# The head of a transformer block: two token tiles multiplied before they are normalised

## The chip, the cores and the metric

The kernel runs on one core of one Trainium2 chip. The metric is the device time of one execution in microseconds (us). Five engines work side by side, each through its own list of instructions in order: TensorE (PE, matrix products and transposes; its weight loads are listed as PEld), VectorE (DVE), ScalarE (ACT), GpSimd (POOL) and SyncE (SP, which here issues most DMA transfers). They wait for each other by semaphores.

## The reference, cut to what matters

One layer of a hybrid block over 1024 tokens of width 1024. Everything that it multiplies first is the RMS-normalised input `h`:

```python
def rmsnorm(x, g):
    xf = x.astype(jnp.float32)
    y = xf * lax.rsqrt(jnp.mean(xf * xf, axis=-1, keepdims=True) + EPS)
    return (y * g.astype(jnp.float32)).astype(x.dtype)
...
    h = rmsnorm(x, norm_g[l])
    proj = h @ w_in[l]
    q, k, v, za, u, vs, zs, gm = jnp.split(proj, IN_SPLITS, axis=-1)
    ...
    sgo = chunked_spatial_gating(jax.nn.gelu(u, approximate=False),
                                 jax.nn.gelu(vs, approximate=False), ...)
```

`h` is x times a gain per column (`norm_g`) times a factor per token (one over the root of the token's mean square). The factor per token can be applied to a row of `h @ w` after the product as well as to the row of `h` before it. The kernel begins with the columns `vs` of the projection.

## The kernel before, in words

Products are made in f32r: each operand is split into a high part, rounded to f32r (a cast on ACT), and a low part, the rest (a subtraction on DVE), and three of the four products of parts are summed in PSUM: high by high, high by low, low by high. A product instruction here is 128 x 128 by 128 x 512.

**The head** is the stretch up to the first large products. Tokens come in eight tiles of 128 (`x[0]` to `x[7]`), loaded by `load_x` into a ring of three buffers (`wr`). `normed_tile(t)` makes a tile of `h`, turned so that the width lies on partitions:

- `scale_of(t)` squares and sums a tile on ACT (L531), and `rstd_of` takes five small steps on DVE (L133 to L145) with a root on ACT between (L135);
- for each half of the width (`j`), L545 on DVE multiplies the tile by the factors and the gain, four transposes on PE (L551) turn it into a PSUM bank (`ps_tp`, two of them), ACT casts the high part (L554), DVE subtracts the low part (L555), and ACT copies the unsplit values (L558, for tile 0 L615) to the places `f11`, `f21`, `f12`, `f22`. From these the sums of a fast (Winograd) scheme are formed later.

The gain is one row, spread over the partitions by two f32 products with ones (L505) into `g_in`, two PSUM banks. `keep_busy` gives PE products of no use (L498) while nothing has arrived.

`vs_gemm(t)` multiplies a tile by the first 512 columns of the `vs` weights: four quarters of weights of 512 KB (`load_vs(c)`, `split_vs(c)`: L582 and L583 for the first, L155 and L156 for the others), 24 products L596 into one bank (`ps_mm`), and L597 on ACT copies the bank to `xh`. Tiles run one after the other: all four quarters for tile 0, then all for tile 1, and so on. `normed_tile(t + 3)` is written behind `vs_gemm(t)`.

Then **the second pass**: the other 512 columns of `vs`, quarter by quarter, each for all eight tiles in eight banks (`vs_step`, 192 products L565). Its weights take `load`, cast and subtraction through the rings `wr`, `wh` and `wl`. `make_forms` builds the operands `t1` to `t4` from the unsplit values beside it, `gelu_of` applies GELU to `xh`. Behind the second pass stand four products for row sums, and then the long sequence of `gemm_pair` (products at L341) that makes up most of the kernel.

**Order.** The text gives a program order; a scheduler then orders each engine's list by its own estimates of when things are ready, so instructions of one tile stand among those of another. `after(second, first)` pins two instructions of one engine. The lists are fixed when the kernel is built: an engine never passes over an instruction that waits. DMA transfers issued by SP go out in SP's order; a load into a ring buffer waits until the readers of what was there have finished.

Of the kernel before, what the change touches and what calls it, by code (L numbers as in the profile page):

```python
# [52 lines left out]
def hybrid_tile(  # L53
# [16 lines left out]
    nc = tc.nc  # L70
# [59 lines left out]
    def rstd_of(ss, scale, base=EPS, n=1):  # L130

        ve = mtile([P, n], F32, f"st{n}", 16 if n == 1 else 5)
        nc.vector.tensor_scalar(ve[:], ss, scale, base, op0=ALU.mult, op1=ALU.add)  # L133
# [11 lines left out]
        nc.vector.tensor_mul(e[:], e[:], r0[:])  # L145
        return e

    def split(hi, lo, src, minus=False):
        if minus:
            nc.scalar.mul(hi, src, -1.0)  # L150
            nc.vector.scalar_tensor_tensor(
                lo, src, -1.0, hi.bitcast(F32), op0=ALU.mult, op1=ALU.subtract
            )
        else:
            nc.scalar.copy(hi, src)  # L155
            return nc.vector.tensor_sub(lo, src, hi.bitcast(F32))  # L156
# [75 lines left out]
    def half_of(half):  # L232
        return slice(half * HALF, (half + 1) * HALF)
# [256 lines left out]
    x_in = {0: load_x(0)}  # L490
    junk = mtile([P, D], F32, "wl", 3)

    ones_r = slot("b22l", (P, HALF))
# [2 lines left out]
    def keep_busy(n):  # L496
        for _ in range(n):
            nc.tensor.matmul(idle[:], ones_r[:, 0:P], ones_r[:], start=True, stop=True)  # L498

    idle = bank("sc")  # L500
    keep_busy(2)

    g_in = [bank("o") for half in range(2)]
    for half in range(2):
        nc.tensor.matmul(g_in[half][:], plain[0:1, 0:P], g_row[:, half_of(half)], start=True, stop=True)  # L505
# [20 lines left out]
    casts = []  # L526

    def scale_of(t):
        xt = x_in[t] if t in x_in else load_x(t)
        ss = mtile([P, 1], F32, "st1", 16)  # L530
        square = nc.scalar.activation(junk[:], xt[:], AF.Square, accum_out=ss[:])  # L531
        if t == 1:

            after(square, casts[-1])
        return xt, rstd_of(ss[:], 1.0 / D)

    def normed_tile(t, scale=None):
        xt, r = scale or scale_of(t)
        if t == 4:
            hb.update(new_b(("b22",)))  # L540
            f.update((n, slot(at, dt=F32)) for n, at in (("f12", "t4h"), ("f22", "t3h")))
        turned = []
        for j in range(2):
            cs = half_of(j)
            nc.vector.scalar_tensor_tensor(  # L545
                xt[:, cs], xt[:, cs], r[:], g_in[j][:], op0=ALU.mult, op1=ALU.mult
            )
            pt = bank("tp")
            for i in range(4):
                k = j * 4 + i  # L550
                nc.tensor.transpose(pt[:, i * P : (i + 1) * P], xt[:, k * P : (k + 1) * P], ident[:])  # L551
            p3 = pt[:].rearrange("p (k c) -> p k c", k=4)
            hi, lo = quarter_of(t, j)
            casts.append(nc.scalar.copy(hi, p3))  # L554
            nc.vector.tensor_sub(lo, p3, hi.bitcast(F32))  # L555
            turned.append((f[f"f{j + 1}{t // 4 + 1}"][:, :, tokens(t)], p3))
            if t:
                nc.scalar.copy(*turned.pop())  # L558
        return turned

    def vs_step(acc, t, k, wh, wl):

# [5 lines left out]
    vs_w = []  # L568

    def load_vs(c):  # L570
        nc.sync.dma_start(vs_raw[c // 2][:, c % 2, :], w[W_VS + c])

    def split_vs(c):

        raw = vs_raw[c // 2][:, c % 2, :].rearrange("p (k n) -> p k n", k=2)
        hi, lo = (v[c // 2][:, 2 * (c % 2) : 2 * (c % 2) + 2, :] for v in vs_split)
        if c:
            split(hi, lo, raw)
        else:

            for k in range(2):
                nc.scalar.copy(hi[:, k, :], raw[:, k, :])  # L582
                (nc.gpsimd if k else nc.vector).tensor_tensor(  # L583
                    lo[:, k, :], raw[:, k, :], hi[:, k, :].bitcast(F32), op=ALU.subtract
                )
        vs_w.extend((hi[:, k, :], lo[:, k, :]) for k in range(2))

    def vs_gemm(t):
        acc = bank("mm")
        for c in range(4):  # L590
            for n in range(3):
                for k in (2 * c, 2 * c + 1):
                    hi, lo = (v[:, k % 4, :] for v in quarter_of(t, k // 4))
                    wh, wl = vs_w[k]
                    lt, rt = ((hi, wh), (hi, wl), (lo, wh))[n]
                    nc.tensor.matmul(acc[:], lt, rt, start=k == 0 and n == 0, stop=k == KC - 1 and n == 2)  # L596
        nc.scalar.copy(xh[:, t, 0:HALF], acc[:])  # L597

    unsplit = normed_tile(0)
    keep_busy(0)  # L600
# [4 lines left out]
    split_vs(0)  # L605
    x_in[1] = load_x(1)
    split_vs(1)
    second = scale_of(1)
    for c in (2, 3):
        load_vs(c)  # L610
    x_in[2] = load_x(2)
    for c in (2, 3):
        split_vs(c)
    for dst, src in unsplit:
        nc.scalar.copy(dst, src)  # L615
    normed_tile(1, second)
    normed_tile(2)
    for t in range(NT):
        vs_gemm(t)
        if t + 3 < NT:  # L620
            normed_tile(t + 3)


    def vs_weights(c):
# [9 lines left out]

    def gelu_of(t):
        two = xh[:, t : t + 2, 0:HALF]
        after(nc.scalar.activation(two, two, AF.Gelu), casts[-1])
        for i in range(2):
            statistics(t + i, 0)

# [38 lines left out]

    mix_w = mtile([P, KC, P], F32, "wT", 1, pool)  # L680
    nc.sync.dma_start(mix_w[:], sg_w)
    nc.vector.memset(mix_w[64:128, :, 0:64], 0.0)
    ones = mtile([P, P], F32R, "ones", 1, pool)
# [1062 lines left out]
```

## Time and profile before

| | us |
|---|---|
| median of 3 runs | 922.93 (922.37 to 922.99) |
| the profiled execution | 923.07 |
| its span | 921.3 |
| PE busy | 904.7 |
| DVE busy | 691.5 |
| ACT busy | 521.8 |
| POOL busy | 126.8 |

The profile is one execution recorded by the hardware. Its page gives busy times and the chain of work that ended last, followed back from the last instruction; the trace behind it answers with timelines (start, length, engine, line, operation, output and inputs, count; in brackets how long the engine had been idle and what ended that) and with waits. Times count from the span's start. Matmuls are pipelined: the length of one is longer than the distance to the next, so pace is read from starts. The granted TensorE clock of the profiled execution is 0.995 of full speed over the span.

### The profile page before, as it was taken

What the parts mean: (1) busy time and instruction counts of PE and PEld (TensorE: products, weight loads), DVE (VectorE), ACT (ScalarE), POOL (GpSimd) and SP (SyncE); (2) the same over time, 40 slices, a digit from 0 to 9 for tenths busy, and PEclk for the clock granted to TensorE, in tenths of its full rate; (3) what the DMA queues carried; (4) which work ended last, traced back from release to release, by engine and by line L of the source; (5) the groups of instructions that cost most, each with busy time, mean ns of one, the idle gap of its engine ahead of it and who ended that gap; (6) DMA issues with size and microseconds to landing.
All of it is one profiled execution on the core that took longest, in us unless ns stands there. A gap on an engine that the chain in (4) does not pass through costs nothing.

```text
span 921.3 us, 13177 instructions
## 1 busy us (share of the span) xinstructions
PE 904.7 (98%) x4332; PEld 752.7 (82%) x4332; DVE 691.5 (75%) x1241; ACT 521.8 (57%) x1046; POOL 126.8 (14%) x188
## 2 busy tenths in 40 slices
PE   8999999999999999999999999999998999999996
PEld 5888888888888788888888888888877887878885
DVE  6875776656687668887778888747798589579996
ACT  6862443334444366767766766755665385367443
POOL 0002122213011001211101111101100111110012
PEclk9999999999999999999999999999999999999998
DMA  6427678877788676776786799689869755998632
GB/s 240 138 91 215 207 197 184 161 158 234 230 290 267 229 200 182 169 202 184 197 240 222 248 220 253 174 313 349 294 219 341 240 201 151 272 307 303 206 115 114
DMA packets 128734, 201.71 MB, mean 219 GB/s; under 512 B 12345, under 2 KB 60729, under 8 KB 128666
## 3 DMA queue, kind: packets, MB, share of 16 engines
q1 hardware_dynamic: 109512, 148.17, 48.8%
q0 software_dynamic: 19008, 52.44, 23.8%
q8 instruction: 34, 0.56, 0.3%
q14 instruction: 34, 0.28, 0.1%
q10 hardware_dynamic: 146, 0.27, 0.1%
HBM read 144.07 MB, written 86.11 MB: 250 GB/s over the span
## 4 chain that ended last, share of the span: by engine, by line
PE 85%; DVE 8%; DMA 4%; issue 2%; ACT 1%; SPq 1%; DVEq 0%; ACTq 0%
PE ps_mm L341 34%; PE ps_o L341 25%; PE ps_mm L596 5%; PE ps_sc L1076 3%; PE ps_o L1161 2%; PE ps_tp L341 2%; PE ps_tp L1120 2%; PE ps_sc L341 2%; PE ps_tp L764 2%; DVE wl L156 1%; PE ps_tp L565 1%; PE ps_sc L565 1%; PE ps_o L565 1%; PE ps_mm L565 1%; DVE bq L185 1%
## 5 line engine op out<-in xcount | busy, mean ns | idle before, releaser
L155 ACT CAST wh<-s 128x1024 fp32r<-128x1024 f32 (+1 forms) x78 | 78.1, 1005 | 87.2 <-PE ps_mm L341 49.9
L156 DVE TENSOR_TENSOR wl<-wr,wh 128x1024 fp32r<-128x1024 f32 (+1 forms) x80 | 75.7, 948 | 49.1 <-ACT wh L155 48.3
L155 ACT CAST wh<-wr 128x1024 fp32r<-128x1024 f32 (+1 forms) x80 | 66.3, 830 | 71.6 <-PE ps_mm L341 34.3
L156 DVE TENSOR_TENSOR wl<-s,wh 128x1024 fp32r<-128x1024 f32 (+1 forms) x78 | 90.9, 1166 | 9.3 <-ACT wh L155 9.2
L341 PE MATMUL ps_o<-T_t1h,wh 128*128 128x512 f32 x148 | 58.9, 398 | 0.8 <-ACT wh L155 0.7
L341 PE MATMUL ps_o<-T_b22h,wh 128*128 128x512 f32 x148 | 58.2, 394 | 0.0
L341 PE MATMUL ps_o<-T_t1h,wl 128*128 128x512 f32 x148 | 57.9, 391 | 0.3 <-DVE wl L156 0.3
L341 PE MATMUL ps_o<-T_b22l,wh 128*128 128x512 f32 x148 | 57.9, 391 | 0.0
L341 PE MATMUL ps_o<-T_b22h,wl 128*128 128x512 f32 x148 | 57.8, 390 | 0.0
L341 PE MATMUL ps_o<-T_t1l,wh 128*128 128x512 f32 x148 | 57.6, 390 | 0.0
L341 PE MATMUL ps_mm<-T_b11h,wl 128*128 128x512 f32 x140 | 54.8, 392 | 2.9 <-DVE wl L156 2.9
L341 PE MATMUL ps_mm<-T_t4h,wh 128*128 128x512 f32 x140 | 55.3, 395 | 0.5 <-DVE x L376 0.5
L341 PE MATMUL ps_mm<-T_t3l,wh 128*128 128x512 f32 x140 | 54.6, 390 | 0.6 <-DVE T_t3l L156 0.6
L341 PE MATMUL ps_mm<-T_t2h,wl 128*128 128x512 f32 x140 | 55.0, 393 | 0.0
L341 PE MATMUL ps_mm<-T_t2l,wh 128*128 128x512 f32 x140 | 55.0, 393 | 0.0
L341 PE MATMUL ps_mm<-T_b11h,wh 128*128 128x512 f32 x140 | 54.9, 392 | 0.0
L341 PE MATMUL ps_mm<-T_t3h,wh 128*128 128x512 f32 x140 | 54.9, 392 | 0.0
L341 PE MATMUL ps_mm<-T_t2h,wh 128*128 128x512 f32 x140 | 54.7, 391 | 0.0
L341 PE MATMUL ps_mm<-T_t4h,wl 128*128 128x512 f32 x140 | 54.7, 391 | 0.0
L341 PE MATMUL ps_mm<-T_t3h,wl 128*128 128x512 f32 x140 | 54.7, 390 | 0.0
L341 PE MATMUL ps_mm<-T_b11l,wh 128*128 128x512 f32 x140 | 54.6, 390 | 0.0
L1089 ACT ACTIVATE pr<-ps_sc,sm 128x192 f32<-128x192 f32 (+2 forms) x128 | 50.9, 410 | 6.5 <-DVE sm L1085 5.5
(356 smaller groups left out, 2399.6 us busy)
## 6 DMA issues: line engine op xcount, KB each, us to landing
wr<-in_w_dram SPq DMA_DIRECT2D x86, 256.0 KB
sums<-in_w_dram POOLq DMA_DIRECT2D x20, 512.0 KB, 5.6
s<-sums SPq DMA_DIRECT2D x20, 512.0 KB
q_hl<-qhl SPq DMA_DIRECT2D x16, 512.0 KB
q<-q_hl SPq DMA_DIRECT2D x64, 128.0 KB
wr<-in_w_dram SPq DMA_DIRECT2D x14, 512.0 KB
y_dr<-x POOLq DMA_DIRECT2D x28, 256.0 KB, 6.6
g<-in_w_dram POOLq DMA_DIRECT2D x12, 512.0 KB, 7.2
```

The costliest lines, as they stand in the source:

```text
L155: nc.scalar.copy(hi, src)
L156: return nc.vector.tensor_sub(lo, src, hi.bitcast(F32))
L185: op(dst[:, i : i + 2, :], a[:, i : i + 2, :], c[:, i : i + 2, :])
L341: nc.tensor.matmul(acc, lt, rt, start=fresh and k == 0 and n == 0, stop=k == 3 and n == 2, skip_group_check=True,)
L565: mm = nc.tensor.matmul(acc, lt, rt, start=k == 0 and n == 0, stop=k == KC - 1 and n == 2)
L596: nc.tensor.matmul(acc[:], lt, rt, start=k == 0 and n == 0, stop=k == KC - 1 and n == 2)
L764: nc.tensor.matmul(pm[:, t * P : (t + 1) * P], xh[:, half * 4 + t, g * P : (g + 1) * P], bias[-1][1][:, g % 4, :], start=True, stop=True,)
L1076: nc.tensor.matmul(sc[:, i, k0:], q_of[:, c, i * P : (i + 1) * P], kt[:, f, k0:], start=f == 0, stop=f == 1,)
L1089: nc.scalar.activation(held_in[c, i], sc[:, i, lo:hi], AF.Exp, bias=nmax[:, c, i : i + 1], scale=-1.0, accum_out=sums[:, c, i : i + 1],)
L1120: nc.tensor.transpose(dst, pr[:, i, block * P : block * P + width], ident[:])
L1161: nc.tensor.matmul(po[:, cs], lt, rt, start=n == 0, stop=n == len(terms) - 1)
```

## The change

The transposes, splits and products of tiles 0 and 1 no longer wait for the tokens' factors. What is turned is `x` itself; the gain, now per partition (`g_cols`, from eight rows of `norm_g` turned on PE), is multiplied in as DVE takes the turned tile from PSUM (`unscaled`). That product is stored unsplit at `f11` and `f21`, and split into the buffers `b12`, which tiles 4 to 7 use later. The products with the `vs` weights are therefore without the tokens' factors; `nc.scalar.mul(xh..., acc, r)` applies these at the copy out of the bank. Tiles 0 and 1 share each quarter of weights in turn, in two banks. Later (`rescaled`, written behind the products of tiles 3 and 4) the stored product is multiplied by the tokens' factors, spread over partitions by an f32 product of ones and a diagonal (`ones32`, `diag`), and split, to give `h` of tiles 0 and 1 for all that follows.

Also: the gain for tiles 2 to 7 is loaded as 128 equal rows into SBUF (`g_in`, 512 KB); the order of loads is x[0], first weights, x[1], second and third weights, gain, x[2], fourth weights; x[0], x[1] and the gain use the ring `wh`; the order of the three products is high by high, low by high, high by low; the first weights' low parts are all on DVE; seven `keep_busy` products come in a row in place of four; a memset of `mix_w` goes from DVE to POOL; the order on ACT and DVE is partly pinned (`in_row`).

```diff
-    g_row = mtile([P, D], F32, "wh", 3)[0:1, :]
-    nc.scalar.dma_start(g_row, norm_g.partition_broadcast(1))
+    g_rows = mtile([P, D], F32, "wl", 3)[0:KC, 0:P]
+    nc.scalar.dma_start(g_rows, norm_g.rearrange("(k p) -> k p", p=P))
...
-    keep_busy(2)
-
-    g_in = [bank("o") for half in range(2)]
-    for half in range(2):
-        nc.tensor.matmul(g_in[half][:], plain[0:1, 0:P], g_row[:, half_of(half)], start=True, stop=True)
-    keep_busy(2)
+    keep_busy(5)
...
+    def turn(t, j):
+
+        pt = bank("tp")
+        for i in range(4):
+            k = j * 4 + i
+            nc.tensor.transpose(pt[:, i * P : (i + 1) * P], x_in[t][:, k * P : (k + 1) * P], ident[:])
+        return pt[:].rearrange("p (k c) -> p k c", k=4)
...
+    def unscaled(t, j):
+
+        p3, v = turn(t, j), whole(t, j)
+        hi, lo = b12[2 * t + j]
+        in_row("D", nc.vector.tensor_mul(v, p3, g_cols[:, 4 * j : 4 * j + 4].unsqueeze(2).broadcast_to([P, 4, P])))
+        yield
+        in_row("A", nc.scalar.copy(hi, v))
+        in_row("D", nc.vector.tensor_sub(lo, v, hi.bitcast(F32)))
+
+    def rescaled(t, r):
+
+        diag = htile([P, P], F32, "diag")
+        after(nc.vector.tensor_scalar_mul(diag[:], ident[:], r[:]), last_of["N"])
+        rb = bank("o")[:, 0:P]
+        nc.tensor.matmul(rb, ones32[:], diag[:], start=True, stop=True)
+        for j in range(2):
+            v = whole(t, j)
+            nc.vector.tensor_mul(v, v, rb.unsqueeze(1).broadcast_to([P, 4, P]))
+            split(*quarter_of(t, j), v)
...
     def normed_tile(t, scale=None):
...
-                xt[:, cs], xt[:, cs], r[:], g_in[j][:], op0=ALU.mult, op1=ALU.mult
+                xt[:, cs], xt[:, cs], r[:], g_in[:, cs], op0=ALU.mult, op1=ALU.mult
...
+    def vs_part(acc, t, c):
+
+        for n in range(3):
+            for k in (2 * c, 2 * c + 1):
...
+                lt, rt = ((hi, wh), (lo, wh), (hi, wl))[n]
+                nc.tensor.matmul(acc, lt, rt, start=k == 0 and n == 0, stop=k == KC - 1 and n == 2)
...
     load_vs(0)
-    load_vs(1)
...
+    nc.sync.dma_start(x_in[1][:], x[P : 2 * P, :])
+    for c in (1, 2):
         load_vs(c)
+    nc.sync.dma_start(g_in[:], norm_g.partition_broadcast(P))
     x_in[2] = load_x(2)
...
+    load_vs(3)
...
+    raws = [unscaled(t, j) for t in range(2) for j in range(2)]
+    parts = split_vs(0)
+    next(raws[0])
+    next(raws[1])
+    keep_busy(2)
+    next(parts)
+    next(raws[0], 0)
+    next(parts, 0)
+    next(raws[1], 0)
+    scales = [scale_of(0)]
+    firsts = [bank("mm") for _ in range(2)]
+    vs_part(firsts[0][:], 0, 0)
+    next(raws[2])
+    next(raws[3])
+    next(raws[2], 0)
+    next(raws[3], 0)
+    vs_part(firsts[1][:], 1, 0)
+    for c in range(1, 4):
+        next(split_vs(c))
+        for t, acc in enumerate(firsts):
+            vs_part(acc[:], t, c)
+    scale = scale_of(2)
+    scales.append(scale_of(1))
+    for t, acc in enumerate(firsts):
+        nc.scalar.mul(xh[:, t, 0:HALF], acc[:], scales[t][1][:])
+        normed_tile(t + 2, None if t else scale)
+    normed_tile(4)
+    for t in range(2, NT):
+        acc = bank("mm")
+        for c in range(4):
+            vs_part(acc[:], t, c)
+        nc.scalar.copy(xh[:, t, 0:HALF], acc[:])
         if t + 3 < NT:
             normed_tile(t + 3)
+        if t in (3, 4):
+            rescaled(t - 3, scales[t - 3][1])
```

In the changed kernel the squares are at L532, the scaling of tiles 2 to 7 at L583, the transposes at L548, the gain products at L559, the products of the first pass at L625 and of the second at L596.

More of the change, by code (lines that the diff above doesn't have):

```diff
@@ L488, in load_x, with htile @@
         return xt
-    x_in = {0: load_x(0)}
+    def htile(shape, dt, tag):
+        return mtile(shape, dt, tag, 1, pool)
+    x_in = {t: mtile([P, D], F32, "wh", 3) for t in range(2)}
+    nc.sync.dma_start(x_in[0][:], x[0:P, :])
+    ones32 = htile([P, P], F32, "ones32")
+    nc.gpsimd.memset(ones32[:], 1.0)
+    g_in = mtile([P, D], F32, "wh", 3)
     junk = mtile([P, D], F32, "wl", 3)
@@ L524, in quarter_of @@
         return [v[:, :, tokens(t)] for v in hb[("b11", "b21", "b22")[j if t < 4 else 2]]]
-    casts = []
     def scale_of(t):
@@ L541, in normed_tile @@
             f.update((n, slot(at, dt=F32)) for n, at in (("f12", "t4h"), ("f22", "t3h")))
-        turned = []
         for j in range(2):
@@ L545, in normed_tile @@
             nc.vector.scalar_tensor_tensor(
-                xt[:, cs], xt[:, cs], r[:], g_in[j][:], op0=ALU.mult, op1=ALU.mult
+                xt[:, cs], xt[:, cs], r[:], g_in[:, cs], op0=ALU.mult, op1=ALU.mult
             )
[L548 to L552, printed above, removed]
-            hi, lo = quarter_of(t, j)
[L554 to L559, printed above, removed]
+            p3 = turn(t, j)
+            hi, lo = quarter_of(t, j)
+            nc.scalar.copy(hi, p3)
+            last_of["N"] = nc.vector.tensor_sub(lo, p3, hi.bitcast(F32))
+            last_of["A"] = nc.scalar.copy(whole(t, j), p3)
     def vs_step(acc, t, k, wh, wl):
@@ L603, in hybrid_tile @@
     load_vs(0)
-    load_vs(1)
[L605 to L609, printed above, removed]
+    nc.sync.dma_start(x_in[1][:], x[P : 2 * P, :])
+    for c in (1, 2):
         load_vs(c)
+    nc.sync.dma_start(g_in[:], norm_g.partition_broadcast(P))
     x_in[2] = load_x(2)
[L612 to L619, printed above, removed]
+    load_vs(3)
+    g_cols = htile([P, KC], F32, "g_cols")
+    pt = bank("tp")
+    nc.tensor.transpose(pt[:, 0:KC], g_rows, ident[0:KC, 0:KC])
+    in_row("D", nc.vector.tensor_copy(g_cols[:], pt[:, 0:KC]))
+    raws = [unscaled(t, j) for t in range(2) for j in range(2)]
[30 more added lines that the diff above has]
+        nc.scalar.copy(xh[:, t, 0:HALF], acc[:])
         if t + 3 < NT:
             normed_tile(t + 3)
+        if t in (3, 4):
+            rescaled(t - 3, scales[t - 3][1])
     def vs_weights(c):
@@ L636, in gelu_of @@
         two = xh[:, t : t + 2, 0:HALF]
-        after(nc.scalar.activation(two, two, AF.Gelu), casts[-1])
+        after(nc.scalar.activation(two, two, AF.Gelu), last_of["A"])
         for i in range(2):
@@ L681, in hybrid_tile @@
     nc.sync.dma_start(mix_w[:], sg_w)
-    nc.vector.memset(mix_w[64:128, :, 0:64], 0.0)
-    ones = mtile([P, P], F32R, "ones", 1, pool)
+    nc.gpsimd.memset(mix_w[64:128, :, 0:64], 0.0)
+    ones = mtile([P, P], F32R, "ones32", 1, pool)
     nc.vector.tensor_scalar(ones[:], ident[:], 0.0, 1.0, op0=ALU.mult, op1=ALU.add)
```

40 lines of the change are left out of this document (18 added, 22 removed).

## The prediction

> **What bounds the kernel now.** I read the page first, then the chain of waits from its start, then the timeline of the first 20 us engine by engine.
>
> ```profile
> span 921.3 us, 13177 instructions
> PE 904.7 (98%) x4332; PEld 752.7 (82%) x4332; DVE 691.5 (75%) x1241; ACT 521.8 (57%) x1046; POOL 126.8 (14%) x188
> ```
>
> TensorE (PE) has work in 98% of the span, so time can only be won where it waits. The chain of waits shows where that is at the head.
>
> ```profile
> 3.99 3.71 PE ps_o L505 x4
> 7.70 0.52 issue
> 8.21 1.94 PE ps_tp L551 x8
> ...
> 18.11 3.70 PE ps_mm L596 x15
> ...
> 62.30 2.72 PE ps_mm L565 x12
> ...
> 103.10 2.72 PE ps_tp L565 x12
> ```
>
> Columns are start, length, what. The first useful PE work is the transposes at 8.21. From 18.11 the chain holds nothing but PE: the head's products (L596) end at 62.30, and the 192 products of the second pass (L565) end at 103.10 + 2.72 = 105.82, at 2.72/12 = 0.227 us each. In the built order of the changed kernel every engine's list after that point is that of before. So I work out when the changed kernel reaches the end of these 192 products; the difference to 105.82 carries to the end unchanged, as later starts hang on the same PE products and copies.
>
> The head in the timeline:
>
> ```profile
> 1.92 2.07 PE L498 MATMUL ps_sc<-T_b22l 128*128 128x512 f32 x4 [1.92 <-DVE T_b22l L494]
> 4.43 1.06 ACT L531 ACTIVATE wl<-wr 128x1024 f32<-128x1024 f32 x1 [1.64 <-DMA wr<-in_x_dram]
> 5.61 0.15 DVE L133 TENSOR_SCALAR st<-st 128x1 f32<-128x1 f32 x1 [3.75 <-ACT wl L531]
> 5.97 1.14 ACT L582 CAST T_t1h<-T_t3h 128x512 fp32r<-128x512 f32 x2
> 6.68 0.16 DVE L145 TENSOR_TENSOR st<-st,st 128x1 f32<-128x1 f32 x1
> 7.37 1.40 DVE L545 SCALAR_TENSOR_TENSOR wr<-wr,st,ps_o 128x512 f32<-128x512 f32 x2
> 7.99 1.05 ACT L155 CAST T_t1h<-T_t3h 128x1024 fp32r<-128x1024 f32 x1 [0.89 <-DMA T_t3h<-in_w_dram]
> 8.21 1.94 PE L551 MATMUL ps_tp<-ident,wr 128*128 128x128 f32 x8 [0.52 <-issue]
> 9.34 0.59 ACT L554 CAST T_b11h<-ps_tp 128x512 fp32r<-128x512 f32 x1 [0.30 <-PE ps_tp L551]
> 9.97 1.22 PE L596 MATMUL ps_mm<-T_t1h,T_b11h 128*128 128x512 f32 x2
> 10.22 0.68 DVE L555 TENSOR_TENSOR T_b11l<-ps_tp,T_b11h 128x512 fp32r<-128x512 f32 x1
> 10.82 0.68 DVE L555 TENSOR_TENSOR T_b21l<-ps_tp,T_b21h 128x512 fp32r<-128x512 f32 x1
> 12.18 0.62 PE L596 MATMUL ps_mm<-T_t1h,T_b11h 128*128 128x512 f32 x2
> 12.64 0.62 PE L596 MATMUL ps_mm<-T_t1l,T_b11h 128*128 128x512 f32 x2
> 12.80 1.23 DVE L156 TENSOR_TENSOR T_t2l<-T_t4h,T_t2h 128x1024 fp32r<-128x1024 f32 x1 [0.79 <-ACT T_t2h L155]
> ```
>
> Read three things. Tile 0 (x[0]) is in SBUF at 4.43, but its transposes wait until 8.21 for its square, the small DVE steps and the scaling L545. One pass of DVE over 512 columns takes 0.60 (10.22 to 10.82), one over 1024 about 1.2. And PE runs at half pace until about 11.5: four fills in 2.0 us, 0.5 apart, eight transposes from 8.21 to 9.97, 0.22 apart, while from 12.18 two products take 0.46 (0.228 each).
>
> **The change, step 1: the start.** It removes L545 for tiles 0 and 1 and the wait for their squares ahead of the transposes. It adds on DVE, before the first products of tile 1, a chain in this built order: gain times transposed tile 0 (two passes), low part of the first weights, of tile 0, of the next weights, of tile 0, one small step, tile 1's pass, small, tile 1's pass, small, tile 1's low part. PE has 7 fills instead of 4: 1.92 + 7 x 0.5 = 5.4, 0.1 for the transposed gain, then tile 0's eight transposes at 0.22 to 7.3. DVE follows the first four as ACT did before (8.21 to 9.34, 1.13): passes start at 6.6 and 7.5. From 7.5 on stand eight passes of 0.6 and three small steps, 0.2 each with the gap, until tile 1's first low part is there: 7.5 + 8 x 0.6 + 3 x 0.2 + 0.1 = 13.0. PE meanwhile has tile 1's transposes when x[1] lands; it is now the third load, and the third of before was there at 7.99. Three of them stand ahead of the first product, which comes near 8.7 instead of 9.97. So the start wins 1.3 us, but at 13.0 PE has done only 8 of the first 48 products: DVE is the bound of this stretch, no longer the square. From there PE has 40 products in a row, the loads being ahead (below): 13.0 + 40 x 0.228 = 22.1. Call it t0: both first tiles multiplied.
>
> Load order: the last quarter of the weights (the eighth load) comes after the gain for 128 partitions and x[2]. Loads of 512 KB pass at 389 GB/s; while the bias, also one row for all partitions, passes, it is 187:
>
> ```profile
> 19.50:20.50 1.00, 1.00 (x6) 0.81 (x5) 0.81 (x5) 1.00 (x3) 0.00 (x0) 1.00 0.98 389
> 20.50:22.00 1.50, 1.50 (x10) 1.16 (x9) 1.46 (x4) 0.42 (x1) 0.00 (x0) 1.00 0.56 187
> ```
>
> The third load is there at 7.99, so the eighth at 7.99 + 5 x 1.35 = 14.7, or 16.1 with the gain at half rate. PE wants its high part at t0 - 12 x 0.228 = 19.4 and ACT needs 1.05: cover of 2 us, cost nothing; landing later than 18.3 would cost PE one for one.
>
> **Step 2: the other tiles.** What the change moves and does not name: in the new ACT order the square of tile t+1 stands behind the two casts and two copies of tile t, and the transposes of t+1 wait for it. Before, PE turned each tile well ahead of need. Rows for that loop:
>
> ```profile
> 16.78 1.20 PE L551 MATMUL ps_tp<-ident,wr 128*128 128x128 f32 x8
> 16.98 0.59 ACT L597 COPY xh<-ps_mm 128x512 f32<-128x512 f32 x1 [1.16 <-PE ps_mm L596]
> 17.46 0.59 ACT L554 CAST T_b11h<-ps_tp 128x512 fp32r<-128x512 f32 x1
> 18.09 0.69 DVE L555 TENSOR_TENSOR T_b11l<-ps_tp,T_b11h 128x512 fp32r<-128x512 f32 x1 [0.82 <-ACT T_b11h L554]
> 18.11 0.73 PE L596 MATMUL ps_mm<-T_t1h,T_b11h 128*128 128x512 f32 x2
> ...
> 34.23 0.63 PE L551 MATMUL ps_tp<-ident,wr 128*128 128x128 f32 x4
> 34.89 0.59 ACT L554 CAST s<-ps_tp 128x512 fp32r<-128x512 f32 x1 [0.25 <-PE ps_tp L551]
> ```
>
> The cast starts 0.66 after the transposes (34.23, 34.89); ACT passes of 512 columns are 0.48 apart (16.98, 17.46); DVE's low part follows its cast at 0.63. From square to next transposes, by tile 0 of before: 4.43 to 6.68, 0.19 to the end of L145, and from L545 to the transposes 7.37 to 8.21, 0.84: 3.28. Followed with these, from t0:
> - Tile 2 is turned only at t0, as tile 1 was at 16.78. PE waits for copy and cast until t0 + 1.31 (18.11 - 16.78 = 1.33 before), of which transposes fill 0.8, then 0.15 for the low part, which the new order hi.wh, lo.wh, hi.wl asks for after two products instead of four: 0.6 lost.
> - ACT: copies of tile 2 until t0 + 3.13, square of tile 3 there, its transposes not before t0 + 6.41; PE gets to them at 6.38. The second half waits 0.3 for L583.
> - Tile 4's square at t0 + 9.89, transposes from 13.17, PE there at 12.85: 0.3 lost. Tile 5's at 16.61, 19.89, PE there at 19.63: 0.3. Tiles 6 and 7 have products of the second pass in front of them in the order and lose 0.2.
>
> Sum 1.7 us of waits. Each turn of the loop is about 6.7 us against 24 x 0.228 + 1.0 = 6.4 of PE work.
>
> **Step 3: the stored product times the factors.** For each of two tiles a 128 x 128 diagonal (DVE 0.2), one f32 product of 128 columns, two DVE passes, two casts, two low parts. The f32 product is on PE: L505 took 3.71/4 = 0.93 per piece of 512 columns at half pace, two pieces each, so 128 columns are 0.23 at full pace; with weight loads I take 0.4 (bounds 0.2 and 0.9), two: 0.8. DVE 2 x (2 x 0.6 + 2 x 0.6) = 4.8 and ACT 2 x 2 x 0.5 lie beside PE's products of tiles 6 and 7: by my following, tile 0's parts are there at t0 + 35 and first read at t0 + 40; tile 1's at 45 and 48. Cost nothing; without that cover PE would wait for the difference.
>
> **The sum.** After t0: 144 products at 0.228 and 192 at 0.227, 76.4; six tiles turned at (62.30 - 18.11 - 168 x 0.228)/6 = 0.98, 5.9; waits 1.7; f32 products 0.8: 84.8. End 22.1 + 84.8 = 106.9 against 105.82: +1.1. The profiled execution took 923.07 us, 921.3 of it span; the median of the three runs, 922.93, lies 0.14 below. So 924.1 there, 924.0 as a time, likely between 923.0 and 925.0. A measurement of this kernel tells about 0.2%, 1.85 us, from no change.
>
> **Where the clock comes in.** The pace of PE doubles near 11.5, though it had been at work from 1.92 to 7.70 with fills and the gain's one-row products, and waited only 0.52. The Trainium skill ("TensorE: Matmul & The Clock Gate", Part 1) says that about 3.4 us of sustained matmuls release the full clock, by a window that runs free. The trace agrees from 8.21 on (3.3 us), and does not for 1.92 to 7.70. The changed kernel fills with 128-row products from 1.92 into the transposes, so by that rule it could be at full pace by about 5.5. What that gives from rows: transposes at 0.1, DVE passes from 6.15 and 6.75 instead of 7.5, t0 = 21.4, end 106.2.
>
> **The rivals.**
> - Full pace early: 923.2, +0.3. For it: no one-row products are left. Against: the 2.0 us of 128-row fills before did nothing visible. Chance 0.22.
> - Slower, the loop: the square-to-transposes path is on PE's path in tiles 3, 4, 5 and partly 7, so each 0.1 us that I have it too short costs 0.4. It decides from 0.3 us longer: 924.0 + 1.2 = 925.2; at 0.5 longer 926.0. For it: ACT and DVE are strictly in order and weights' casts stand between; the load of w behind tile 5 lands with almost no slack. Against: durations are from undisturbed rows. Chance 0.30.
> - Faster: PE finds its tiles scaled as before (no step 2 waits beyond the first 0.6: -1.1), full pace early (-0.7), f32 products at 0.2 (-0.4), and DVE's gain passes overlapping more with the low parts (-0.7): 921.1. For it: chain of before shows no waits once tiles run ahead. Against: the new ACT order. Chance 0.13.
> - That the change doesn't do what it says: the built order has the transposes ahead of any scaling, so no chance is kept.
>
> **How the numbers follow.** The forecast, half pace until about 11.5 and 1.7 of waits, has 0.35; it and early pace lie within 0.2% of 922.93. Of the loop's 0.30 nearly all is over 924.78, with none of the rest. Of the faster case about all is under 921.08. Range for 8 in 10: from 921.3, just short of the faster case, to 926.2, the loop at 0.55 longer.
>
> **What would show it.** Right: first L625 product near 8.7; tile 1's first low part (x) near 12.3 to 13.0, and PE waiting for DVE before it; both first tiles done near 22; PE waits ahead of the transposes of tiles 3 to 5 named L583; second pass done near 106.9. Wrong: transposes at 0.1 before 8 us, or waits ahead of transposes missing or over 0.6, or a stretch after 107 us whose length is not that of before.

## The result, and the profile after

The changed kernel took 928.89 us (median of 4 runs, 927.11 to 929.69) where the kernel before took 922.96 (4 runs, 922.37 to 923.65): 1.0053 times as long, 95% interval 1.0039 to 1.0068. The forecast was 924.0 with a range up to 926.2, so it is wrong by 4.9 us, and the kernel became slower than the range allowed for. The profiled execution took 928.54 us.

The page of the changed kernel shows the same picture as before, with 5.5 us more span and PE as busy as it was:

```profile
span 926.8 us, 13193 instructions
PE 905.4 (98%) x4336; PEld 754.0 (81%) x4336; DVE 697.5 (75%) x1252; ACT 522.8 (56%) x1046; POOL 126.5 (14%) x189
```

The chain of waits from 10 us on (start, length, what) shows the difference:

```profile
10.59 10.84 DMA sink_sb<-in_sinks_dram
...
21.52 0.09 DVE nsink_sb L772
21.61 0.04 issue
21.66 0.75 DVE wr L583
...
23.28 0.64 PE ps_tp L548 x4
23.92 0.02 issue
23.94 0.69 ACT xh L664
24.62 0.48 ACT T_b11h L588
25.11 0.04 issue
25.15 4.91 PE ps_mm L625 x13
```

In the kernel before, this chain held nothing but PE from 18.11 on. Now a transfer stands in it that neither the diff nor the prediction speaks of: the load of the sinks, 16 numbers that attention needs after 300 us. DVE negates them in L772 (L718 before), and DVE works strictly in order, so tile 2's scaling L583 stands behind it. In the timeline of DVE (start, length, instruction; in brackets the idle time before it and what ended it):

```profile
18.66 0.16 DVE L145 TENSOR_TENSOR st<-st,st 128x1 f32<-128x1 f32 x1
21.52 0.17 DVE L772 TENSOR_SCALAR nsink_sb<-sink_sb 128x8 f32<-128x8 f32 x1 [2.70 <-DMA sink_sb<-in_sinks_dram]
21.66 0.75 DVE L583 SCALAR_TENSOR_TENSOR wr<-wr,st,wh 128x512 f32<-128x512 f32 x1
```

The factor of tile 2 is ready at 18.82, and its scaling starts at 21.66. In the kernel before, the same instruction stood one step earlier in DVE's list, ahead of the last step of tile 2's factor (L145), and the load was there when DVE came to it. DVE's rows, and PE's row for tile 2's transposes:

```profile
20.31 0.16 DVE L718 TENSOR_SCALAR nsink_sb<-sink_sb 128x8 f32<-128x8 f32 x1
20.43 0.16 DVE L145 TENSOR_TENSOR st<-st,st 128x1 f32<-128x1 f32 x1
20.62 1.41 DVE L545 SCALAR_TENSOR_TENSOR wr<-wr,st,ps_o 128x512 f32<-128x512 f32 x2
21.64 0.61 PE L551 MATMUL ps_tp<-ident,wr 128*128 128x128 f32 x4
```

There it cost nothing. PE's list had 15 of tile 1's products ahead of tile 2's transposes, from 18.11 on, and PE came to these at 21.64, some 0.3 us after the first half of the scaling was done (20.62 and half of 1.41). In the changed kernel both first tiles are multiplied at 21.8, and tile 2's transposes are the next thing in PE's list. Beside that, DVE now comes to the negation at 18.82 instead of 20.31, and eleven loads of 512 KB stand ahead of the sinks in SP's order where nine stood: the gain's rows and x[4] are new there. So the change does act on this load, though no line of the diff names it. PE then waits twice, and after that it runs at half pace. Its rows, and the granted clock (last but two) in stretches of 2 us:

```profile
21.21 0.61 PE L625 MATMUL ps_mm<-T_t2l,s 128*128 128x512 f32 x2
22.51 1.40 PE L548 MATMUL ps_tp<-ident,wr 128*128 128x128 f32 x8 [0.69 <-PE ps_mm L625]
25.15 0.97 PE L625 MATMUL ps_mm<-T_t1h,T_b11h 128*128 128x512 f32 x2 [1.25 <-ACT T_b11h L588]
25.93 1.18 PE L625 MATMUL ps_mm<-T_t1h,T_b11l 128*128 128x512 f32 x2
26.90 1.05 PE L625 MATMUL ps_mm<-T_t1l,T_b11h 128*128 128x512 f32 x2
```

```profile
24.00:26.00 2.00, 0.85 (x3) 0.42 (x3) 0.87 (x2) 1.73 (x4) 0.00 (x0) 0.87 0.47 143
26.00:28.00 2.00, 2.00 (x6) 1.61 (x6) 0.42 (x1) 1.99 (x4) 0.00 (x0) 0.50 0.30 119
28.00:30.00 2.00, 2.00 (x8) 1.59 (x8) 1.47 (x6) 0.29 (x2) 0.00 (x0) 0.78 0.00 0
```

The first wait is put down to PE's own products; what really ended it is the scaling L583, whose first half was done at 22.41. The second pair of tile 2's products starts at 25.93 and the third at 26.90: 0.4 to 0.5 us a product where 0.228 is the full pace.

The second wait ends with ACT's cast of tile 2 (L588). Ahead of it in ACT's list stands the copy L664 of tile 1's bank, which needs tile 1's factor, and DVE's steps for that factor stand behind the negation as well:

```profile
23.68 0.16 DVE L145 TENSOR_TENSOR st<-st,st 128x1 f32<-128x1 f32 x1
23.94 0.69 ACT L664 ACTIVATE xh<-ps_mm,st 128x512 f32<-128x512 f32 x1 [0.65 <-PE ps_tp L548]
```

The profile puts the wait of this copy down to the transposes, but the copy reads nothing of them; what it reads last is the factor (`st`), ready at 23.84. So the one instruction holds up two things that PE needs.

In the chain the second pass ends where the row sums (L766) start. It did so at 105.82 before; now:

```profile
110.20 0.93 PE ps_sc L766 x4
```

That is 4.4 us later, against the 1.1 us predicted. At a later DMA transfer, of q_hl (294.83 against 290.31), it is still 4.5.

### The profile page after: what moved, and what is told of

Its sections match the earlier page's. It is cut to its first block, busy times and chain, and to the rows that moved or that the text cites. A ratio compares the mean times of both kernels' runs of the same rounds, so it can differ in the third digit from the quotient of the medians.

```text
span 926.8 us, 13193 instructions
## 1 busy us (share of the span) xinstructions
PE 905.4 (98%) x4336; PEld 754.0 (81%) x4336; DVE 697.5 (75%) x1252; ACT 522.8 (56%) x1046; POOL 126.5 (14%) x189
## 4 chain that ended last, share of the span: by engine, by line
PE 83%; DVE 7%; DMA 6%; ACT 2%; issue 1%; SPq 1%; DVEq 0%; ACTq 0%
PE ps_mm L341 35%; PE ps_o L341 26%; PE ps_sc L1130 3%; PE ps_mm L625 3%; PE ps_o L1215 2%; PE ps_sc L341 2%; PE ps_tp L341 2%; PE ps_tp L1174 2%; PE ps_tp L818 2%; DMA wr<-in_w_dram 1%; PE ps_sc L596 1%; PE ps_mm L596 1%; PE ps_tp L596 1%; PE ps_o L596 1%; DMA sink_sb<-in_sinks_dram 1%
## 5 line engine op out<-in xcount | busy, mean ns | idle before, releaser
L341 PE MATMUL ps_mm<-T_t4l,wh 128*128 128x512 f32 x140 | 55.1, 393 | 0.0
```

The lines of the kernel that those rows point to most:

```text
L341: nc.tensor.matmul(acc, lt, rt, start=fresh and k == 0 and n == 0, stop=k == 3 and n == 2, skip_group_check=True,)
```

## The experiments

The theory: DVE's wait for the sinks' load, and the clock that falls in PE's gap behind it, are the 3.3 us that the prediction lacks. Each ratio below is to the kernel before, with its 95% interval. "Start" is tile 2's first product, "end" the end of the second pass, both in us of the profiled execution.

**Move the one instruction.** The negation is pinned behind an instruction at 90 us:

```
-    nc.vector.tensor_scalar_mul(nsink_sb[:], sink_sb[:], -1.0)
+    after(nc.vector.tensor_scalar_mul(nsink_sb[:], sink_sb[:], -1.0), low)
```

> The changed kernel with one DVE instruction pinned later in DVE's order: the negation of the sinks (L772), which stood between tile 2's rstd and tile 2's scaling, now stands behind the low part of the mixing weights, after 90 us. Nothing else moves. Theory (the wait of this instruction for the sinks' load holds tile 2's scaling, and the gap on PE that follows lets the clock fall): the scaling L583 starts near 18.9 instead of 21.66, tile 2's products start near t0 + 1.3 = 23.0 instead of 25.15, the clock stays at 1.00 between 25 and 30, the second pass ends 3.5 to 4.0 us earlier, time 924.9 to 925.4 against 928.9. Rival A (another late step takes its place, such as r of tile 1 ahead of the copies L664, or the gain's load): at most 1.5 us won, 927.4 or more. Rival B (the clock falls there anyway): 2.2 us won, 926.7.

Measured: 1.0029 (1.0018 to 1.0041); start 23.29, end 107.10. The granted clock is 1.00 from 8 to 30 us, and of PE's waits one of 0.38 us is left:

```profile
18.12 0.75 DVE L583 SCALAR_TENSOR_TENSOR wr<-wr,st,wh 128x512 f32<-128x512 f32 x1
21.87 1.04 PE L548 MATMUL ps_tp<-ident,wr 128*128 128x128 f32 x8
23.29 0.73 PE L625 MATMUL ps_mm<-T_t1h,T_b11h 128*128 128x512 f32 x2 [0.38 <-ACT T_b11h L588]
...
107.10 0.93 PE ps_sc L766 x4
```

The same kernel a second time:

> The kernel with the negation of the sinks moved late, once more: its profiled execution took 924.6 us, but the median of its six runs was 927.0. Theory P (what differs from run to run is whether the clock falls after the two gaps on PE near 325 and 700 us, some 1.6 us each time): the head is that of the first profile to 0.3 us, second pass done at 107.1, and the difference between the executions is found in these two places. Rival W (the last quarter of the weights lands up to 4 us later in some runs, as in the run with the sinks loaded early, and PE waits for it in the head): second pass done at 108 to 110 in a slow execution, with a wait of PE for ACT's cast of T_t4h before 22 us.

Measured: 1.0015 (1.0006 to 1.0024); start 22.80, end 106.64. The changed kernel was taken again too:

> The changed kernel once more, unchanged, beside the experiments on one chip. Theory (the sinks' load holds tile 2's scaling): again a wait of 2 to 3 us ahead of the negation of the sinks, tile 2's products near 25, second pass done near 110, time 4.5 to 6 us above the kernel before. If that wait was an accident of one profiled execution, it is gone here and the time lies near that of the kernel with the negation moved late (2.7 us above before).

Measured: 1.0044 (1.0029 to 1.0058); DVE waits 3.64 us for the sinks, start 24.68, end 110.06. So in both pairs the move wins 3.1 to 3.4 us at the end of the second pass (3.5 to 4.0 expected), and 0.0024 to 0.0029 of the time (2.2 to 2.7 us). From tile 1's last product to tile 2's first the changed kernel takes 3.3 and 3.4 us, with the negation late 1.3 us both times. Rival A falls, since no other late step takes the place. Rival B had 2.2 us as its price, which the time alone would fit; it falls by the clock, which stays at 1.00 without the gap.

The weights were early in both executions with the negation late (rival W not seen). Theory P isn't borne out by this pair either: the second execution took 2.1 us longer, but in both the clock fell near 700 us and not near 325. What differs is the way from the second pass to PE's first product behind the transfer of z_dr, near 325: 218.1 and 220.6 us, with transfers in it that took longer (q_hl 5.49 and 6.95 us).

**Fill the gap.** To part the clock from the wait, eight products that nobody reads were put in PE's gap, the wait left alone:

```
+        if (t, j) == (2, 0):
+            fill(3, last_of["P"])
...
+        if (t, j) == (2, 1):
+            fill(5, last_of["P"])
```

> The changed kernel with the sinks' wait left as it is, and eight fill products of 512 columns (1.83 us of PE) put into the gap on PE that follows it: three between tile 1's last product and tile 2's transposes, five between these transposes and tile 2's first product. Theory (the gap of PE itself makes the clock fall): tile 2's products still start near 25.2, but at 0.23 us each from the first on, and the second pass ends 1.0 to 1.8 us earlier (tile 3's transposes are now reached before their scaling and wait up to 0.7), time 927.1 to 927.9. Rival B (the clock falls there for another reason): products at 0.43 as before, 928.9; if the fills stand in the way, up to 929.5.

Measured: 1.0061 (1.0047 to 1.0074); start 25.43, end 109.66. The granted clock in the stretch that was 0.50:

```profile
26.00:28.00 2.00, 2.00 (x9) 1.54 (x9) 0.70 (x2) 1.86 (x3) 0.00 (x0) 1.00 0.51 184
```

So it is the idle time that lets the clock fall. From start to end the changed kernel takes 85.05 and 85.38 us (its two profiles), the one with the gap filled 84.23, and the two profiles with the negation late 83.81 and 83.84. Of the 3.1 to 3.4 us, 1.9 is the later start (25.15 to 23.29, 24.68 to 22.80) and 1.2 to 1.5 is the slower road from there; with the gap filled 0.8 to 1.2 of these are gone, so most of it is the clock. The fill gave back less than the 1.7 us that the low clock had cost by an estimate from the stretches (2 us times 0.13, 0.50 and 0.22), as tile 3's transposes are then reached before their scaling and wait 0.58 (none in the changed kernel; the built order also has them three products earlier). The second pass ends 0.4 to 0.5 us earlier, where 1.0 to 1.8 were expected, and in the time nothing was won: this expectation is missed, though the clock did what it says.

**Load the sinks early, by another queue.**

```
+    for e in range(2):
+        nc.scalar.dma_start(sink_sb[...], of_head[e].partition_broadcast(64))   # at the very start
```

> The changed kernel with the two loads of the sinks issued by ACT at the start, right behind its first activation, instead of by SP as twelfth and thirteenth load. The negation stays in its place on DVE, ahead of tile 2's scaling. Theory (the late landing of this load is what DVE waits for): the sinks are in SBUF before 18.8, the instruction stands without a wait, and the time is that of the kernel with the instruction moved, 924.9 to 925.4. Rival C (what holds DVE there is not the sinks' load but something else named by its semaphore): no change, 928.9. If these small loads take over 10 us wherever they are issued, they still land near 13.

Measured: 1.0053 (1.0032 to 1.0074); start 25.64, end 109.44. DVE no longer waits for the sinks, so rival C falls. But now PE and DVE wait for ACT's cast of the weights' last quarter, and the time is no better:

```profile
18.65 1.05 ACT L624 CAST T_t2h<-T_t4h 128x1024 fp32r<-128x1024 f32 x1 [3.78 <-DMA T_t4h<-in_w_dram]
```

That cast started at 15.38 in the changed kernel: with 4 KB of sinks ahead, the loads of 0.5 MB land 3.3 us later. This was in no theory, and raised the question of what is slow in that load: its place in the queue or its shape.

**Shape and place.** The load writes pairs of numbers: 512 pieces of 8 B. One kernel loads whole rows, 128 pieces of 64 B, from the same place in the queue; the other keeps the pieces and issues them ahead of x[3], x[4] and the mixing weights.

```
-            sink_sb[e * 64 : (e + 1) * 64].rearrange("p (c r) -> p c r", r=2), of_head[e].partition_broadcast(64)
+    nc.sync.dma_start(sink_row[:], sinks.partition_broadcast(P))
```

> The changed kernel with the negation left ahead of tile 2's scaling, and the sinks loaded from the same place in SP's order in another shape: all 16 values to each of 128 partitions (128 pieces of 64 B) instead of every second pair to 64 partitions, twice (512 pieces of 8 B). The negation reads this row, in two steps of 64 partitions; GpSimd copies the rest. Theory S (the many small pieces take the time: in the two traces of the changed kernel the DMA rate is 16 to 83 GB/s for 3 to 4 us behind the large loads): the row lands within 1 us of the load of the mixing weights before it, near 18.5; DVE waits at most 1 us, PE not at all, second pass done at 106.6 to 107.2, time that of the kernel with the negation late (1.0015 to 1.003 of before). Rival Q (it is the place behind x[3], x[4] and the mixing weights in the queue): it still lands after 20.5 and nothing is won.

> The changed kernel with the negation left ahead of tile 2's scaling, and the two loads of the sinks, in their old shape, issued by SP ahead of x[3], x[4] and the mixing weights (1.5 MB, 3.9 us at 400 GB/s) instead of behind them. Theory Q (the place in the queue): landed near 17.5, no wait, second pass done at 106.6 to 107.2. Theory S (the 512 small pieces themselves take 4 us, and what stands behind them in the queue waits): landed near 18 to 19, a wait of up to 1 us, x[3] some 3 us later than before, near 20; tile 3's square then starts when ACT gets to it, near 25, so no cost; the same 106.6 to 107.5. If both come out without a wait, place and pieces each carry part of it.

Whole rows: 1.0001 (0.9985 to 1.0017), start 23.41, end 107.23. Small pieces, but earlier: 1.0018 (1.0005 to 1.0031), start 22.97, end 106.91. DVE's waits, first of the whole rows, then of the earlier pieces:

```profile
18.82 0.44 DVE L773 TENSOR_SCALAR nsink_sb<-sink_row 64x8 f32<-64x8 f32 x1 [1.28 <-DMA sink_row<-in_sinks_dram]
```

```profile
18.05 0.17 DVE L587 TENSOR_SCALAR nsink_sb<-sink_sb 128x8 f32<-128x8 f32 x1 [0.21 <-DMA sink_sb<-in_sinks_dram]
```

The stretches show what the pieces do (last two columns: busy share of the DMA engines, GB/s). With the earlier pieces:

```profile
11.00:13.00 2.00, 1.38 (x5) 0.86 (x6) 2.00 (x6) 1.96 (x3) 0.00 (x0) 1.00 1.04 424
13.00:14.00 1.00, 1.00 (x6) 0.79 (x5) 0.82 (x2) 1.00 (x2) 0.00 (x0) 1.00 0.41 113
14.00:16.00 2.00, 2.00 (x11) 1.65 (x10) 2.00 (x3) 1.87 (x3) 0.00 (x0) 1.00 0.03 1
16.00:17.00 1.00, 1.00 (x6) 0.83 (x5) 0.77 (x2) 0.55 (x4) 0.00 (x0) 1.00 0.14 38
17.00:19.00 2.00, 2.00 (x10) 1.67 (x9) 1.65 (x8) 1.05 (x3) 0.00 (x0) 1.00 0.96 391
```

For about 3 us next to nothing moves, though the DMA engines are hardly busy, and the large loads behind the pieces stand still. In the changed kernel this falls behind the large loads:

```profile
16.00:17.00 1.00, 1.00 (x6) 0.84 (x5) 0.54 (x1) 1.00 (x2) 0.00 (x0) 1.00 1.03 422
17.00:19.00 2.00, 2.00 (x11) 1.65 (x10) 1.45 (x6) 1.69 (x5) 0.00 (x0) 1.00 0.27 66
```

Both theories hold a part: the place puts the pieces behind 1.5 MB (until 17), the shape adds 4.4 us (17 to the landing at 21.43). Taking away either brings the end of the second pass to where the late negation has it. For the whole rows that is in part luck. DVE still waits 1.28 us, which makes tile 1's factor late again, and PE waits for it, where the expectation had no wait:

```profile
23.41 0.73 PE L625 MATMUL ps_mm<-T_t1h,T_b11h 128*128 128x512 f32 x2 [1.25 <-ACT T_b11h L588]
```

From tile 1's last product to tile 2's first it takes 2.2 us there, against 1.3 with the earlier pieces; but tile 1 was done at 21.2 us, some 0.5 earlier than there. The times differ by more than the ends do; in the two profiles the clock fell near 325 us with the earlier pieces and not with the whole rows (more on this below).

**The loop.** From tile 3 on each square goes one tile further ahead in ACT's order; the negation is late here too:

```
     for t, acc in enumerate(firsts):
         nc.scalar.mul(xh[:, t, 0:HALF], acc[:], scales[t][1][:])
-        normed_tile(t + 2, None if t else scale)
-    normed_tile(4)
+        ahead[t + 3] = scale_of(t + 3)
+        normed_tile(t + 2, ahead[t + 2])
+    ahead[5] = scale_of(5)
+    normed_tile(4, ahead[4])
```

> The changed kernel with the negation of the sinks moved late, and from tile 3 on the square of each tile one tile further ahead in ACT's order (tile 3's ahead of the copies of the first two products, tile 4's ahead of tile 3's scaling, and so on). Theory (step 2 of the prediction is right that transposes wait for the square, and the sinks were the rest): against the kernel with only the negation moved another 0.7 to 1.1 us is won, waits ahead of the transposes of tiles 4 and 5 are gone, time 923.9 to 924.6. Rival D (the waits of the loop are hidden or something else on ACT, such as the casts behind the earlier square, becomes late): no difference to the kernel with only the negation moved, or up to 0.5 us slower.

Measured: 1.0003 (0.9993 to 1.0014); start 23.24, end 106.21. The waits ahead of the transposes of tiles 4 and 5, 0.39 and 0.36 with the negation late, are gone, and the second pass ends 0.4 to 0.9 us earlier (0.7 to 1.1 expected); a new wait of 0.40 us, for tile 2's low part, stands at 24.38. Rival D falls.

**Tile 2 ahead of tile 1's last products.** Its eight transposes are emitted before the last six products of tile 1, in addition to the above:

> The kernel with the negation late and the squares one tile further ahead, and beside that tile 2 turned before the last 6 products of tile 1 instead of behind them, so that its cast and low part lie beside these products. Theory (what is left of the loss is the wait between tile 1's last product and tile 2's): tile 2's products follow tile 1's without a wait, 0.8 to 1.2 us won, second pass done at 105.0 to 105.4 against 106.2 without it and 105.8 in the kernel before; time 922.9 to 923.4 where before takes 923.9. Rival (the copies out of the first two banks, now behind tile 2's casts on ACT, or the transposes in front of tile 1's products, hold PE instead): no change, 924.0 or up to 0.5 more.

> The kernel with the negation late, the squares one tile ahead and tile 2 turned before tile 1's last products, once more, since its second pass was done 1.0 us earlier than in the kernel before while its time was the same within 1.2 us. If the head's gain comes through to the end: 0.9 to 1.2 us under the kernel before, 0.999. If it is lost again later (the q_hl transfer took 7.6 us instead of 5.6, and the clock fell after both later gaps on PE): same time, 1.000, with the loss at the same places in the trace.

Measured: 0.9997 (0.9985 to 1.0010) and 0.9998 (0.9983 to 1.0012); start 22.39 in the first, end 104.83 and 104.73. The second pass now ends 1.0 to 1.4 us earlier than in the kernel before (105.82 and 106.10), a little more than expected, and the time is the same: no version here beats the kernel before by more than its interval. In the two profiles the gain is lost on the way from the second pass to PE's first product behind the transfer of z_dr: 220.8 and 223.4 us, against 217.7 and 218.6 in the two profiles of the kernel before. In the second the chain holds four transfers of q_hl between 274.5 and 302 us, where that of the changed kernel had one at 294.83. But these two executions took 926.41 and 929.05 us where the medians of their kernels were 923.72 and 924.10, so they don't show where an execution of median length loses the microsecond, and why the transfers take longer was not settled.

**Order of the loads, and the later stretch.**

> The kernel with the negation of the sinks late, with SP's loads reordered: the last quarter of the weights as sixth load, then x[2], then the gain for 128 partitions (in the changed kernel: gain, x[2], last quarter). Rival W of the run before (late weights make the slow executions): the median falls from 927.0 to 924.5, and the executions lie within 1.5 us of each other. Theory P (clock falls in the later gaps): no change in median or spread, 926 to 927. If the gain, now last, lands after 18 us, tile 2's scaling waits for it and the time is up to 1 us longer.

Measured: 1.0025 (1.0012 to 1.0037), start 22.58, end 106.47, median 927.04, runs from 924.36 to 930.15. Neither median nor spread became smaller, and rival W falls; that fits what theory P expected of this run.

> The kernel before, once more with a profile, since its one trace shows a stretch from 105.8 to the end of 815.5 us, where the other kernels took 815.7 to 819.8 with the same instructions. If that is chance (the clock falls or not after the gaps near 325 and 700, q_hl's transfer takes 4.6 to 7.6 us): a stretch of 815 to 819 here too, and the second pass done at 105.8 within 0.6. If the change slows the later stretches: 815.5 again.

Measured: 1.0000 (0.9988 to 1.0013), end 106.10, and 815.8 us from there to the end of the span, 815.5 in the first profile. For the changed kernel and those derived from it this stretch, with the same instructions in the same order, took 815.7 to 818.8 us, and with tile 2 early 819.8 and 822.5. So the stretch is not one number: part of what the second pass wins or loses is given back or added later. The theory of chance is not shown, though. 815.8 is nearer to the 815.5 of the other theory, and of the fourteen stretches the two of the kernel before are the shortest and the third shortest. That the change itself lengthens what follows is not excluded.

## Why the prediction was wrong, step by step

**The step that failed** is step 2's first line: "Tile 2 is turned only at t0", with the copy, the cast and the low part as all that PE would wait for: first product at t0 + 1.31, 0.6 us lost. It took tile 2's scaling, and tile 1's factor for the copy, as done by then. The path was followed from the square on, but not along DVE's list, where the built order has the negation of the sinks between tile 2's factor and its scaling. Measured from the end of tile 1's products, the first product of tile 2 came 3.3 and 3.4 us later in the changed kernel, and 1.3 us later in both profiles with the negation late: the line holds to 0.1 us as soon as this one instruction is out of the way. The load behind it was visible in the trace of before, issued at 11.08 and used at 20.31, 1.5 us behind the time at which the changed kernel wants it. The prediction had asked of the last quarter of the weights and of the gain when they land, but not of this load, since no line of the diff names it. Measured, the place of this 0.17 us instruction cost 1.9 us of start and 1.2 to 1.5 us of the way from there.

Of the 4.9 us between forecast and time, 3.3 stand at the end of the second pass and are this term. Another 1.1 came between there and the end of the span; for these no cause is shown.

**What the change itself takes away is cover.** In the kernel before most of tile 1's products stood in PE's list ahead of tile 2's transposes; in the changed one the first two tiles are consumed together and PE has none left when tile 2 is due. No rival named this: the slower rival had the square's path in the loop as its mechanism, and 926.0 as its price.

**Step 1, the start.** Half pace until 11.5 was taken, full pace early was a rival, and the rival is what came at first:

```profile
5.29 1.09 PE L548 MATMUL ps_tp<-ident,wh 128*128 128x128 f32 x8
...
8.22 0.71 PE L548 MATMUL ps_tp<-ident,wh 128*128 128x128 f32 x3 [1.83 <-DMA wh<-in_x_dram]
8.58 1.20 PE L625 MATMUL ps_mm<-T_t1h,s 128*128 128x512 f32 x2
```

The transposes are 0.1 apart, as the Trainium skill ("TensorE: Matmul & The Clock Gate", Part 1) would have it after some 3.4 us of products. Then PE waits 1.83 us for x[1], and the two products at 8.58 are 0.5 apart again. The first product comes at 8.58 (predicted 8.7), tile 1's first low part is there at 12.31 (13.0), both first tiles are done at 21.8 (22.1, or 21.4 with early pace). The number was right to 0.3 us, in part by luck: transposes at 0.1 before 8 us were the prediction's own sign of being wrong, and what they won was lost again in the fall of the clock behind x[1]. PE, slow until about 11.5, reached tile 1's low part after it was there. In the profiles in which the clock stayed up PE did wait for this chain, as the step says (1.31 us at 11.87 with the negation late, first profile), and both tiles were done between 21.2 and 22.0. Full pace didn't come at one time: in that profile tile 0's and tile 1's first transposes are still 0.22 apart (eleven in 2.47 us from 5.40), and in one of the twelve profiles of the changed kernel and those derived from it, tile 2 early the second time, half pace lasted to 11.3. The last quarter of the weights landed at 15.4 (14.7 to 16.1) and hid as said.

**The rest of step 2.** The waits ahead of the transposes named L583 came as predicted, 0.30 and 0.38 for tiles 4 and 5 in the changed kernel (0.3 each predicted), none for tiles 3, 6 and 7 (0.3 and 0.2 predicted). With the negation late, tile 4:

```profile
35.35 0.63 PE L548 MATMUL ps_tp<-ident,wr 128*128 128x128 f32 x4 [0.39 <-DVE wr L583]
```

**Step 3.** Right in kind: an f32 product takes 0.22 of PE in the chain, where 0.4 was taken and 0.2 was the lower bound, and the DVE passes that follow lie beside PE's products:

```profile
57.42 0.22 PE ps_o L569 x2
57.64 0.93 PE ps_mm L625 x4
```

**The sum.** 106.9 was predicted for the end of the second pass. With the one instruction out of the way it is 107.10 and 106.64, and from the end of tile 1's products to there 85.1 us in both (84.8 predicted). So the rest of the sum stands, and the missed term is the whole of the error there. In the time these kernels are 1.0015 to 1.0029 of before, 1.4 to 2.7 us, of which the second pass accounts for 0.5 to 1.3 us; the rest is not explained.

**"The difference to 105.82 carries to the end unchanged."** True for the changed kernel within 1.1 us (4.4 at the second pass, 5.5 in the span). Over all runs it is not a law: the version with the head 1.0 us faster ended no earlier.

## What to carry to other kernels

Before a change that makes the tensor engine consume its work in hand faster, list everything that stands in the in-order queues of the engines that feed it, in the built order, and ask of each whether its input is there by the new time. An instruction that costs nothing in the trace of before has a price once its cover is gone or its input comes later, and it needn't be one that the diff touches. A step whose result is needed much later is best pinned late, and a load of a few bytes is worth its shape: whole rows, not pairs.

## What the runs showed of the hardware that was not expected

Small pieces stop the large loads. With 4 KB in 512 pieces of 8 B on their way, next to nothing moved for about 3 us (1 GB/s from 14 to 16 us above, with a DMA share of only 0.03), between stretches of 424 and 391 GB/s. The same numbers in 128 pieces of 64 B were used at 18.82 instead of 21.52.

Idle stretches of PE well under 3 us let the clock fall. The waits of 0.69 and 1.25 us around eight transposes were enough, in both profiles of the changed kernel, and so was the 1.83 us for x[1]. The Trainium skill ("TensorE: Matmul & The Clock Gate", "HAM oscillation") gives gaps above some 3.4 us as the rule; the trace doesn't agree, shorter ones do it. But not each: waits of 1.24 and 1.26 us for x[1] (gap filled, whole rows) left the clock up, and so did the 1.25 us ahead of tile 2 with whole rows. In the head the stretch without any product but transposes parts the cases: 3.3 us and more where the clock fell (from 5.20 to 8.58 and from 21.82 to 25.15 in the changed kernel), under 3.3 where it stayed up. Whether transposes count less than products is not shown by this, and near 700 us two waits of 0.7 and 1.7 us between products were enough. That the window runs free (the same page, Part 1) would fit what two later places show. PE has much the same waits near 325 and 700 in every profile, but the granted clock differs. Kernel before, first and second profile:

```profile
318.00:334.00 16.00, 14.60 (x68) 11.82 (x68) 9.71 (x29) 8.77 (x30) 0.00 (x0) 0.89 0.77 223
696.00:712.00 16.00, 13.56 (x59) 10.59 (x58) 12.36 (x15) 6.26 (x11) 2.16 (x4) 1.00 1.02 375
```

```profile
318.00:334.00 16.00, 14.16 (x75) 11.74 (x75) 9.60 (x28) 9.17 (x30) 0.00 (x0) 1.00 0.80 234
696.00:712.00 16.00, 13.55 (x53) 10.79 (x53) 12.07 (x15) 4.79 (x8) 2.16 (x4) 0.89 1.01 365
```

A mean of 0.89 over 16 us is 1.8 us less of full clock. Over the 14 profiles it fell near 325 in 7 and near 700 in 13. The way from the products near 325 to those near 700 us takes 376.1 to 376.3 us where it fell near 325 and 374.1 to 374.7 where it didn't. The way from the second pass to 325 varies more, from 217.7 to 223.4 us, with the transfers in it. This spread is as large as the effects measured here, so the end of the second pass was the better gauge of the head.
